# A gated decoder block: the positions' transfer, filler products, modulation rows, weight sums and gate constants in another order

## The chip, the core and the metric

One core of one Trainium2 chip runs the whole block as one program. TensorE (PE) multiplies, VectorE (DVE), ScalarE (ACT) and GpSimd (POOL) do elementwise work, and transfers between HBM and the core's SBUF are issued from the queues of SyncE (SP), ACT and POOL. Each engine takes its instructions strictly in the order of the program. The metric is the device time of one execution in microseconds.

## What is computed

The input is 2048 tokens of width 1024 in float32. Cut to what matters:

```python
c_act = silu(c)
shift, scale, gate = split(c_act @ w_ada + b_ada, 3)
h = rms(x, g_pre) * (1 + scale) + shift
q, k, v, z_a, u_b, v_b, z_b, g_logits = split(h @ w_in, ...)     # 4608 columns
q, k = rope(q, positions), rope(k, positions)
y_a = sliding_window_attention(q, k, v, sinks) * silu(z_a)       # window 128
y_b = gelu(u_b) * spatial_gating(layernorm(gelu(v_b))) * silu(z_b)
merged = sigmoid(g_a) * (y_a @ w_proj_a) + sigmoid(g_b) * (y_b @ w_proj_b)
out = x + gate * rms(merged @ w_out, g_post)
```

`rms` divides each token's row by its root mean square.

## The kernel before

The three large products (`w_in`, the two projections, `w_out`) are done by a two-level scheme of seven products in place of eight: an operand is cut into quarters A11, A12, A21, A22, and four sums of quarters, S1 = A21 + A22, S2 = S1 - A11, S3 = A11 - A21, S4 = A12 - S2, enter beside the quarters. Each quarter or sum is split into a high and a low half, and each product is three passes (high by high, high by low, low by high) of `mm3` (line 164). For a weight the high half is ACT's cast (line 212) and the low half DVE's subtraction (line 147). For an activation (the tiles T) ACT's copy (lines 638 and 640) makes the high half and DVE (lines 147 and 647) the low one.

`run_all` goes through the program in slots, one product of one block of weights to a slot. `later(n, f)` puts f a number of slots later, before or after that slot's product. Work on weights is a stream: `loads` are transfers, `sums` the sums of quarters, `preps` the casts. `want(n)` brings the stream up to cast n; before each cast it issues loads, makes the low half that is still due (`low_now`) and makes the sums up to that place. So the order on ACT and DVE follows from these calls, and each engine keeps it.

The first three blocks of weights (NFIRST) run together, product by product, so their first 21 slots are product 0 of block 0, 1, 2, then product 1 of block 0, 1, 2, and so on. Product 1 uses S1, product 2 uses S2, product 4 uses S3, product 5 uses S4. For these blocks `combos` makes the sums on DVE, for later ones on POOL. Each sum is also stored to HBM (`keep`), for the second half of the tokens.

Ahead of the first slot stands the prologue, for the first 512 tokens. `positions` spreads the positions over the partitions by a product with the identity (line 570, into bankY; the casts and copies for it are lines 568 and 569), and `rope_do(n)` does the next n of 25 steps on DVE that lead to sine and cosine. `squares` takes squares on ACT (536, 539) and sums them on DVE (153); `rstd` sums over partitions on TensorE (551, into bankZ), copies the result (554, DVE) and takes the inverse root on POOL (143, 144); `rstd_out` spreads it over the partitions (560, into bankW). `ada_row(0, kks)` multiplies the modulation weights of row kk (585), `ada_rows_out` copies the result (591, ACT), and `ada_fin` turns it (597, TensorE) and makes the factors A and offsets SH (603 to 606, DVE). Then come the activations (574, 640, 647) and the first `mm3`. `warm(n)` are filler products whose result nobody reads (425). Product 1's activations (T_365), those for tokens 512 to 1023, need a second norm and a second set of rows (`second_half`, after slot 2); `ada_fin(1)` stands in the middle of slot 3.

The sine and the cosine need another table on ACT (lines 510 and 518) than the GELU of line 745; each change is an ACT_TABLE_LOAD.

On ACT's queue the constants `col` and `cst` go out first (121, 128); the positions (449) stand behind the activation of line 419, which needs `col`. SP's queue carries the activations, the modulation weights and the first weights in this order, up to 40 us.

Late in the first product, with the second half of the tokens, `gate_end(h)` (slots 87 and 91) loads two rows of constants (1089, 1090) into buffers of the kind S, of which there are four, and lines 1099 and 1100 use them. In the same slots `o_step` (1069) loads pieces of `w_out` and has POOL make sums of them in S buffers, and attention loads its queries and keys (921, 924) for the scores of lines 940 and 941. There are ten buffers of the kind x.

Of the kernel before, what the change touches and what calls it, by code (L numbers as in the profile page):

```python
# [8 lines left out]
F32 = mybir.dt.float32  # L9
F32R = mybir.dt.float32r  # L10
I32 = mybir.dt.int32
# [8 lines left out]
NG = 4  # L20
# [35 lines left out]
def hybrid_block(ctx: ExitStack, tc: tile.TileContext, xt, x, wada, wgate, wI, wP, wO,  # L56
# [33 lines left out]
    def const(shape, name, dt=F32):  # L90
        return cp.tile(shape, dt, tag=name, name=name)
# [26 lines left out]


    col = const([P, 48], "col")[:, 0:NCOL]  # L120
    act.dma_start(col, colc)
# [78 lines left out]
    def w_get():  # L200
        n = taken[0]
        taken[0] += 1
        want(min(n + LA, max(2 * n - 2, NFIRST - 1)))
        if n + LA >= len(preps):
            low_now()
        w = ready[n]
        ready[n] = None
        return w
# [30 lines left out]
    def combos(env, n, first):  # L239

        def keep(i, t):
            if n is not None:
                later(1, lambda: sp.dma_start(sS[n][i], t))

        second = sub if first else psub

        def s13():
            s1 = env["S1"] = flat("S")
            if first:
                add(s1, env["A21"], env["A22"])  # L250
            else:
                psub(s1, env["A21"], env["A22"], ALU.add)
            second(env["A21"], env["A11"], env["A21"])
            keep(0, s1)
            keep(2, env["A21"])

        def s2():
            second(env["A11"], env["S1"], env["A11"])
            keep(1, env["A11"])

        def s4():
            low_now()
            second(env["A12"], env["A12"], env["A11"])
            keep(3, env["A12"])

        sums.extend([[], [s13, s2], [], [], [s4], [], []] if first else [[s13], [], [s2], [], [s4], [], []])
        preps.extend([lambda k=k: env[k] for k in ("A11", "S1", "A11", "A12", "A21", "A12", "A22")])

    def stream_fresh(quads, n=None):
# [4 lines left out]
        if first:  # L274
            plan.append((6, "A22", "raw"))
        for off, key, tag in plan:
            loads.append((at + off, fetch(env, key, quads[key], tag)))
        combos(env, n, first)
# [149 lines left out]
    adaw = [[T_new(F32).rearrange("p (a b) -> p a b", a=4) for _ in range(2)] for _ in range(2)]  # L428
    ropew = T_new(F32).rearrange("p (a b) -> p a b", a=8)
    rg = const([P, D], "rg")  # L430
# [16 lines left out]

    posi = ropew[0:NG, 7, :].bitcast(I32)
    act.dma_start(posi, pos)
    x_load(0)  # L450
# [209 lines left out]
    T[0], T[1] = t_new(), t_new()  # L660
    warm(2)
    positions()
    rope_do(6)
    squares(0, range(KT))
    warm(8)
    ada_row(0, range(0, 1))
    rstd(0, BK["Z"])
    ada_row(0, range(1, 2))
    rstd_out(0, BK["W"])
    rope_do(10)  # L670
    ada_row(0, range(2, 8))
    want(1)
    low_now()
    ada_load(1)
    cur["cap"] = 10
    ada_rows_out(0)
# [409 lines left out]
    def gate_end(h):  # L1086
        sl = slice(h * 512, (h + 1) * 512)
        bg, gp = flat("S"), flat("S")
        sp.dma_start(bg, rowc[0:1, sl].broadcast_to([P, 512]))
# [41 lines left out]
    def run_all():  # L1131
        nonlocal T

        for s in range(NS):
# [34 lines left out]
            if s == 0:  # L1169
# [4 lines left out]
                def second_half():  # L1174
                    rstd(1, BK["Z"])
                    ada_row(1, range(2))
                    rstd_out(1, BK["W"])
                    sum_to(NFIRST + 1)
                    want(NFIRST)
                    for i in range(6):  # L1180
                        t_part(1, i)
                        if i == 2:
                            low_now()
                    ada_row(1, range(2, 8))
                    ada_rows_out(1)
# [4 lines left out]
                later(2, second_half, True)  # L1190
                later(4, fetch_all, True)
                later(3, lambda: ada_fin(1), "mid")
# [201 lines left out]
```

## Time and profile before

| | us |
|---|---|
| median of 3 runs | 1241.12 |
| lowest and highest | 1240.72, 1242.14 |
| profiled execution, its own time | 1238.44 |
| its span, first to last instruction | 1236.7 |
| PE busy in the span | 1206.4 (98%) |
| DVE busy | 832.9 (67%) |
| ACT busy | 610.9 (49%) |
| POOL busy | 271.2 (22%) |

Times in the timeline count from the start of the span. A row gives start, duration, engine, line, operation, output and inputs by the program's names, and in brackets how long the engine stood before it and what ended that. "SPq" and "ACTq" are issues of transfers. A float32 product appears as passes: each filler of `warm` as two. "PEclk", the granted clock, is 1.00 at full speed and 0.50 at half.

### The profile page before, as it was taken

How to read it: one execution, taken by the hardware profiler on the slowest of the kernel's cores; microseconds unless marked ns; L12 is line 12 of the kernel's file. 1: busy time of each engine (PE TensorE's matmuls, PEld its weight loads, DVE VectorE, ACT ScalarE, POOL GpSimd, SP SyncE). 2: the span in 40 equal slices, each digit the busy share in tenths (PEclk: the TensorE clock that was granted, in tenths of full speed). 3: DMA queues.
4: the chain of work that ended last, by engine and by line, in shares of the span. 5: the costliest groups of instructions: out<-in, count | busy, mean ns of one | idle time of the engine just before them, and what ended most of it. 6: DMA issues, size and time to landing. Idle time of an engine off the chain costs nothing.

```text
span 1236.7 us, 17163 instructions
## 1 busy us (share of the span) xinstructions
PE 1206.4 (98%) x5500; PEld 960.7 (78%) x5500; DVE 832.9 (67%) x1290; ACT 610.9 (49%) x1324; POOL 271.2 (22%) x243
## 2 busy tenths in 40 slices
PE   8888999999999999999999999999999999999997
PEld 3566888887777777888888787777788888888886
DVE  5897688577777677348765775465746557677775
ACT  2366444576765667444344675455722112444443
POOL 0001556223465300013300001221000000135342
PEclk8999999999999999999999999999999999999999
DMA  9344898867999988468787666998787677754552
GB/s 362 128 138 146 296 335 295 257 180 218 279 334 342 316 294 281 141 217 290 263 278 199 175 171 186 332 282 257 263 290 237 223 244 242 266 184 143 164 179 85
DMA packets 215506, 294.15 MB, mean 238 GB/s; under 512 B 19828, under 2 KB 96244, under 8 KB 215416
## 3 DMA queue, kind: packets, MB, share of 16 engines
q1 hardware_dynamic: 214944, 292.37, 73.1%
q8 instruction: 43, 0.70, 0.2%
q0 software_dynamic: 176, 0.53, 0.2%
q14 instruction: 47, 0.39, 0.1%
q10 hardware_dynamic: 296, 0.16, 0.0%
HBM read 189.50 MB, written 98.24 MB: 233 GB/s over the span
## 4 chain that ended last, share of the span: by engine, by line
PE 86%; DVE 5%; DMA 4%; ACT 2%; issue 2%; SPq 1%; POOL 1%; DVEq 0%; ACTq 0%; POOLq 0%
PE bankY L164 27%; PE bankX L164 19%; PE bankZ L164 12%; PE bankW L164 12%; PE s L164 4%; PE b L164 4%; PE b L990 2%; PE s L940 1%; DMA T<-in_wada 1%; PE s L941 1%; PE b L879 1%; PE b L975 1%; DVE W L147 1%; DMA T<-in_xt 0%; DVE T L647 0%
## 5 line engine op out<-in xcount | busy, mean ns | idle before, releaser
L164 PE MATMUL bankY<-T,W 128*128 128x512 f32 x1608 | 390.4, 391 | 1.4 <-ACT bankZ L409 1.1
L164 PEld LDWEIGHTS bankY<-T,W 128*128 128x128 f32 x1608 | 299.5, 188 | 64.7 <-ACT bankZ L409 1.5
L147 DVE TENSOR_TENSOR W<-raw,W 128x512 fp32r<-128x512 f32 x323 | 237.7, 743 | 74.2 <-ACT W L212 72.1
L164 PE MATMUL bankX<-T,W 128*128 128x512 f32 x1140 | 279.4, 393 | 1.7 <-DVE T L647 1.3
L212 ACT CAST W<-raw 128x512 fp32r<-128x512 f32 x323 | 199.2, 617 | 152.2 <-PE b L164 48.4
L164 PEld LDWEIGHTS bankX<-T,W 128*128 128x128 f32 x1140 | 211.3, 188 | 47.4 <-DVE T L647 3.6
L164 PE MATMUL bankW<-T,W 128*128 128x512 f32 x708 | 177.9, 398 | 8.0 <-DVE W L147 3.7
L164 PE MATMUL bankZ<-T,W 128*128 128x512 f32 x708 | 173.2, 394 | 0.9 <-DVE W L147 0.9
L164 PEld LDWEIGHTS bankW<-T,W 128*128 128x128 f32 x708 | 132.3, 191 | 40.4 <-DVE W L147 4.2
L164 PEld LDWEIGHTS bankZ<-T,W 128*128 128x128 f32 x708 | 133.6, 190 | 29.2 <-DVE W L147 1.5
L150 POOL TENSOR_TENSOR S<-raw,raw 128x512 f32<-128x512 f32 x22 | 29.5, 1339 | 275.3 <-DMA raw<-m 201.3
L150 POOL TENSOR_TENSOR raw<-raw,raw 128x512 f32<-128x512 f32 x44 | 67.2, 1528 | 89.2 <-DVE W L147 42.1
L153 DVE TENSOR_TENSOR e<-bankY,e 128x512 f32<-128x512 f32 x41 | 28.3, 690 | 65.5 <-PE bankY L164 65.4
L147 DVE TENSOR_TENSOR T<-x,T 128x512 fp32r<-128x512 f32 (+1 forms) x93 | 64.5, 736 | 9.6 <-ACT T L364 9.1
L164 PE MATMUL s<-T,W 128*128 128x512 f32 x276 | 66.4, 389 | 0.0
L150 POOL TENSOR_TENSOR S<-x,x 128x512 f32<-128x512 f32 x18 | 26.1, 1459 | 182.6 <-DMA x<-in_wO 174.9
L150 POOL TENSOR_TENSOR raw<-S,raw 128x512 f32<-128x512 f32 x22 | 32.8, 1490 | 138.5 <-DVE W L147 115.1
L164 PEld LDWEIGHTS s<-T,W 128*128 128x128 f32 x276 | 51.7, 188 | 10.7
L364 ACT CAST T<-x 128x512 fp32r<-128x512 f32 x88 | 48.8, 618 | 4.2 <-PE s L164 4.2
L969 ACT ACTIVATE P<-P,rc 128x128 f32<-128x128 f32 x128 | 44.4, 396 | 11.3 <-DVE rc L965 11.0
L409 ACT COPY bankZ<-bankY 128x512 f32<-128x512 f32 x42 | 24.0, 570 | 52.7 <-PE bankY L164 52.6
L388 ACT COPY e<-bankW 128x512 f32<-128x512 f32 x41 | 24.0, 584 | 52.1 <-PE bankW L164 49.5
(233 smaller groups left out, 1405.3 us busy)
## 6 DMA issues: line engine op xcount, KB each, us to landing
raw<-in_wI SPq DMA_DIRECT2D x128, 256.0 KB, 4.6
raw<-sS SPq DMA_DIRECT2D x84, 256.0 KB, 4.6
g<-e SPq DMA_DIRECT2D x64, 256.0 KB, 4.4
sS<-raw SPq DMA_DIRECT2D x48, 256.0 KB, 4.0
T<-in_wada SPq DMA_DIRECT2D x16, 512.0 KB, 8.1
q<-q SPq DMA_DIRECT2D x64, 128.0 KB, 5.2
q<-k_s SPq DMA_DIRECT2D x64, 128.0 KB, 4.7
raw<-in_wP SPq DMA_DIRECT2D x32, 256.0 KB, 3.3
```

The costliest lines, as they stand in the source:

```text
L147: dve.tensor_tensor(out=o, in0=a, in1=b, op=ALU.subtract)
L150: pool.tensor_tensor(out=o, in0=a, in1=b, op=op)
L153: dve.tensor_tensor(out=o, in0=a, in1=b, op=ALU.add)
L164: pe.matmul(o, w[:, i, sl], t[:, j, kt, :], start=start and kt == kts[0] and n == 0, stop=stop and kt == last and n == 2, skip_group_check ...
L212: act.copy(w[:, 0, :], src)
L364: act.copy(T[p][:, 0, kt, :], rs[kt])
L388: act.copy(self.wsb, b["W"])
L409: act.copy(self.b[to], self.b[of])
L879: pe.matmul(b[:, ch * P : (ch + 1) * P], st["v", h][:, ch, :], wT[:, c, :], start=True, stop=True)
L940: pe.matmul(o, q[:, g, :], k[:, 0, :], start=True, stop=False)
L969: act.activation(out=st["P", kv][:, g, 0:P], in_=st["P", kv][:, g, 0:P], func=AF.Copy, scale=st["rc", kv][:, g : g + 1])
L990: pe.matmul(o[own, :], v[:, k, own], st["pv", kv][k], start=k == 1, stop=k == 0)
```

## The change

Six things are edited; no arithmetic is added or dropped.

1. The positions' transfer becomes the first on ACT's queue, ahead of `col` and `cst`; its tile is allocated earlier, so tiles carry other numbers.
2. Three fillers stand before the positions' product and six after it, instead of two and eight.
3. Two more rope steps follow the squares, and eleven instead of ten follow the norm: 19 of the 25 are done before the first product instead of 16.
4. Three modulation rows instead of two stand before `rstd_out`.
5. For the first three blocks S1 is made first for all of them, ahead of product 1's activations; S2 and S3, which were made with it, follow with products 1 to 4. S2 no longer overwrites A11 but A22, which makes A22 be loaded again under the name A22b, and S3 overwrites A21 later. `w_get` makes the due low half at once for casts 3 to 5, `want(NFIRST + 1)` is called inside the making of product 1's activations, and two limits on loads (`cap`, `fetch_all`) change.
6. `gate_end` takes x buffers instead of S.

```diff
+    ropew = T_new(F32).rearrange("p (a b) -> p a b", a=8)
+    posi = ropew[0:NG, 7, :].bitcast(I32)
+    act.dma_start(posi, pos)
     col = const([P, 48], "col")[:, 0:NCOL]
     act.dma_start(col, colc)
...
         want(min(n + LA, max(2 * n - 2, NFIRST - 1)))
+        if NFIRST <= n < 2 * NFIRST:
+            low_now()
...
-        def s13():
-            s1 = env["S1"] = flat("S")
-            if first:
-                add(s1, env["A21"], env["A22"])
-            else:
-                psub(s1, env["A21"], env["A22"], ALU.add)
+
+        two = "A22" if first else "A11"
+
+        def s1():
+            env["S1"] = flat("S")
+            (add if first else lambda o, a, b: psub(o, a, b, ALU.add))(env["S1"], env["A21"], env["A22"])
+            keep(0, env["S1"])
+
+        def s3():
             second(env["A21"], env["A11"], env["A21"])
-            keep(0, s1)
             keep(2, env["A21"])
 
         def s2():
-            second(env["A11"], env["S1"], env["A11"])
-            keep(1, env["A11"])
+            env["S2"] = env[two]
+            second(env["S2"], env["S1"], env["A11"])
+            keep(1, env["S2"])
...
-        sums.extend([[], [s13, s2], [], [], [s4], [], []] if first else [[s13], [], [s2], [], [s4], [], []])
+        sums.extend([[], [s1], [s2], [], [s3], [s4], []] if first else [[s1, s3], [], [s2], [], [s4], [], []])
...
-            plan.append((6, "A22", "raw"))
+            plan.append((6, "A22b", "raw"))
...
-    posi = ropew[0:NG, 7, :].bitcast(I32)
-    act.dma_start(posi, pos)
...
-    warm(2)
+    warm(3)
     positions()
     rope_do(6)
     squares(0, range(KT))
-    warm(8)
+    rope_do(2)
+    warm(6)
     ada_row(0, range(0, 1))
     rstd(0, BK["Z"])
-    ada_row(0, range(1, 2))
+    ada_row(0, range(1, 3))
     rstd_out(0, BK["W"])
-    rope_do(10)
-    ada_row(0, range(2, 8))
+    rope_do(11)
+    ada_row(0, range(3, 8))
...
-    cur["cap"] = 10
+    cur["cap"] = 8
...
-        bg, gp = flat("S"), flat("S")
+        bg, gp = flat("x"), flat("x")
...
-                    sum_to(NFIRST + 1)
+                    sum_to(2 * NFIRST)
                     want(NFIRST)
                     for i in range(6):
                         t_part(1, i)
                         if i == 2:
                             low_now()
+                        elif i == 4:
+                            want(NFIRST + 1)
...
-                later(4, fetch_all, True)
+                later(3, fetch_all, True)
```

TensorE in the prologue, before; line 425 is the filler, 570 the positions' product, 585 the modulation rows (two instructions each), 551 the norm's partition sums, 560 its spreading:

```order
L425 MATMUL bankX<-ones 128x512 x2
L570 MATMUL bankY<-T_320 128x512
L425 MATMUL bankX<-ones 128x512 x8
L585 MATMUL b_408<-T_316,cact 64x512 x2
L551 MATMUL bankZ<-ones,e_377 128x2 x4
L585 MATMUL b_408<-T_316,cact 64x512 x2
L560 MATMUL bankW<-cst,rs_417 128x128 x4
L585 MATMUL b_408<-T_316,cact 64x512 x4
L585 MATMUL b_408<-T_317,cact 64x512 x8
```

The same place now, the lines being 436, 578, 593, 559 and 568:

```order
L436 MATMUL bankX<-ones 128x512 x3
L578 MATMUL bankY<-T_291 128x512
L436 MATMUL bankX<-ones 128x512 x6
L593 MATMUL b_409<-T_318,cact 64x512 x2
L559 MATMUL bankZ<-ones,e_378 128x2 x4
L593 MATMUL b_409<-T_318,cact 64x512 x4
L568 MATMUL bankW<-cst,rs_418 128x128 x4
L593 MATMUL b_409<-T_318,cact 64x512 x2
L593 MATMUL b_409<-T_319,cact 64x512 x8
```

One filler has moved ahead of the positions' product and one is gone; one row has moved from behind the spreading to before it.

DVE after product 1's last activation, before; 153 and 147 on S and raw are the sums of blocks 1 and 2, 603 to 606 the second factors, 147 on W the weights' low halves, 574 the scaling of product 2's activations:

```order
L147 TENSOR_TENSOR T_365<-Tt,T_365 128x512
L153 TENSOR_TENSOR S_625<-raw_497,P_499 128x512
L147 TENSOR_TENSOR raw_497<-raw_352,raw_497 128x512
L147 TENSOR_TENSOR raw_352<-S_625,raw_352 128x512
L153 TENSOR_TENSOR S_631<-raw_501,S_503 128x512
L147 TENSOR_TENSOR raw_501<-raw_354,raw_501 128x512
L147 TENSOR_TENSOR raw_354<-S_631,raw_354 128x512
L603 TENSOR_TENSOR AS<-b_648,col 128x4
...
L147 TENSOR_TENSOR W_629<-S_625,W_629 128x512
L147 TENSOR_TENSOR W_667<-S_631,W_667 128x512
L574 SCALAR_TENSOR_TENSOR x_325<-x_325,AS,e_586 128x512
```

The same place now (W_614, W_663 are the weights of blocks 1 and 2 for product 1, W_669 that of block 0 for product 2, P_497 and P_501 are S2 of blocks 0 and 1):

```order
L150 TENSOR_TENSOR T_365<-Tt,T_365 128x512
L150 TENSOR_TENSOR W_614<-S_592,W_614 128x512
L611 TENSOR_TENSOR AS<-b_643,col 128x4
...
L150 TENSOR_TENSOR P_497<-S_590,raw_350 128x512
L150 TENSOR_TENSOR W_663<-S_594,W_663 128x512
L150 TENSOR_TENSOR P_501<-S_592,raw_352 128x512
L150 TENSOR_TENSOR W_669<-P_497,W_669 128x512
L582 SCALAR_TENSOR_TENSOR x_326<-x_326,AS,e_588 128x512
```

Six sums have gone from between the activations and the factors; two other sums and the subtraction for W_669 have come ahead of the scalings.

ACT at that place, before; 638 and 212 are casts of activations and weights, 591 copies the second modulation rows, 388 and 409 copy banks after product 1 of block 0:

```order
L638 CAST T_365<-Tt 128x512
L591 COPY e_623<-b_577 128x512
L212 CAST W_629<-S_625 128x512
L388 COPY m_663<-bankW 128x512
L409 COPY bankW<-bankX 128x512
L212 CAST W_667<-S_631 128x512
L212 CAST W_672<-raw_350 128x512
```

And now:

```order
L646 CAST T_365<-Tt 128x512
L217 CAST W_614<-S_592 128x512
L599 COPY e_629<-b_579 128x512
L399 COPY m_658<-bankW 128x512
L420 COPY bankW<-bankX 128x512
L217 CAST W_663<-S_594 128x512
L217 CAST W_669<-P_497 128x512
```

The cast of block 1's weights has moved ahead of the copy of the rows; the cast of block 2's stands where it stood, behind the two copies of banks.

Further on, ACT's sine comes during product 3 and its cosine during product 4, instead of products 4 and 5, so that four table loads follow the first one instead of five. On SP's queue the instructions around `gate_end` keep their order; only the buffers' names change, from S to x.

More of the change, by code (lines that the diff above doesn't have):

```diff
@@ L245, in combos, with last @@
         second = sub if first else psub
-        def s13():
-            s1 = env["S1"] = flat("S")
-            if first:
-                add(s1, env["A21"], env["A22"])
-            else:
-                psub(s1, env["A21"], env["A22"], ALU.add)
+        two = "A22" if first else "A11"
[4 more added lines that the diff above has]
+        def s3():
             second(env["A21"], env["A11"], env["A21"])
-            keep(0, s1)
             keep(2, env["A21"])
         def s2():
-            second(env["A11"], env["S1"], env["A11"])
-            keep(1, env["A11"])
+            env["S2"] = env[two]
+            second(env["S2"], env["S1"], env["A11"])
+            keep(1, env["S2"])
         def s4():
             low_now()
-            second(env["A12"], env["A12"], env["A11"])
+            second(env["A12"], env["A12"], env["S2"])
             keep(3, env["A12"])
-        sums.extend([[], [s13, s2], [], [], [s4], [], []] if first else [[s13], [], [s2], [], [s4], [], []])
-        preps.extend([lambda k=k: env[k] for k in ("A11", "S1", "A11", "A12", "A21", "A12", "A22")])
+        def last():
+            return env["A22b"] if first else env["A22"]
+        sums.extend([[], [s1], [s2], [], [s3], [s4], []] if first else [[s1, s3], [], [s2], [], [s4], [], []])
+        preps.extend([lambda k=k: env[k] for k in ("A11", "S1", "S2", "A12", "A21", "A12")] + [last])
     def stream_fresh(quads, n=None):
@@ L274, in stream_fresh @@
         if first:
-            plan.append((6, "A22", "raw"))
+            plan.append((6, "A22b", "raw"))
         for off, key, tag in plan:
-            loads.append((at + off, fetch(env, key, quads[key], tag)))
+            loads.append((at + off, fetch(env, key, quads[key[:3]], tag)))
         combos(env, n, first)
@@ L428, in hybrid_block @@
     adaw = [[T_new(F32).rearrange("p (a b) -> p a b", a=4) for _ in range(2)] for _ in range(2)]
-    ropew = T_new(F32).rearrange("p (a b) -> p a b", a=8)
     rg = const([P, D], "rg")
```

## The prediction

> **What bounds the kernel now.** I read the page first, then the waits, then the timeline of the stretches in which TensorE stands. From the page, the span and the chain of work that ended last:
>
> ```profile
> span 1236.7 us, 17163 instructions
> ...
> PE 86%; DVE 5%; DMA 4%; ACT 2%; issue 2%; SPq 1%; POOL 1%; DVEq 0%; ACTq 0%; POOLq 0%
> ```
>
> TensorE sets the end. The change leaves out no product, so it can gain only where TensorE does not yet run its products back to back (the first 118 us), or stands later. The list of waits, TensorE only, from 110 us to the end (waited for; us in total, times, longest), has five entries; the longest:
>
> ```profile
> PE s L940 <- DMA q<-k_s: 2.5, 1, 2.5
> ```
>
> It is one wait of 2.5 us, and it is of interest below. All else is decided before 118 us. The timeline there (start, duration, engine, line, in brackets the idle time before):
>
> ```profile
> 1.11 3.51 PE L425 MATMUL bankX<-ones 128*128 128x512 f32 x4 [1.11 <-DVE nhalf L126]
> ...
> 3.84 0.51 ACTq L449 DMA_DIRECT2D T<-in_pos  x1
> ...
> 7.39 0.42 DVE L568 CAST T<-T 4x512 f32<-4x512 int32 x1 [2.94 <-DMA T<-in_pos]
> ...
> 7.99 2.07 PE L570 MATMUL bankY<-T 4*128 4x512 f32 x2 [3.38 <-DVE T L569]
> ...
> 9.99 9.33 PE L425 MATMUL bankX<-ones 128*128 128x512 f32 x16
> 10.10 0.75 DVE L461 TENSOR_SCALAR T<-bankY,col 128x512 f32<-128x512 f32 x1 [2.16 <-PE bankY L570]
> ...
> 13.34 5.46 DVE L153 TENSOR_TENSOR e<-e,m 128x512 f32<-128x512 f32 x7
> ...
> 19.25 1.08 PE L585 MATMUL b<-T,cact 128*64 128x512 f32 x4
> ...
> 20.26 1.05 PE L551 MATMUL bankZ<-ones,e 128*128 128x2 f32 x8
> ...
> 21.35 0.16 DVE L554 COPY ss<-bankZ 128x4 f32<-128x4 f32 x1 [2.55 <-PE bankZ L551]
> ...
> 23.50 1.16 PE L560 MATMUL bankW<-cst,rs 128*128 128x128 f32 x8 [1.18 <-POOL rs L144]
> ...
> 24.59 5.37 PE L585 MATMUL b<-T,cact 128*64 128x512 f32 x24
> ...
> 30.01 0.59 ACT L591 COPY e<-b 128x512 f32<-128x512 f32 x1 [3.69 <-PE b L585]
> ...
> 31.74 0.16 DVE L603 TENSOR_TENSOR AS<-b,col 128x4 f32<-128x4 f32 x1 [2.93 <-PE b L597]
> ```
>
> It is one chain: positions land, a matmul spreads them, DVE does six rope steps and seven sums of squares (10.10 to 18.80), TensorE sums over partitions (20.26), POOL takes the root, TensorE spreads it (23.50), the last six modulation rows follow, and only then (31.74) are there weights for the activations.
>
> **The positions' transfer.** Now it is issued at 3.84, behind an activation that waits for the constants. First on the queue it goes out some 3 us earlier, and the two other transfers one place (0.45 us) later. From the table of DMA issues (size, us from issue to landing):
>
> ```profile
> cst<-in_consts ACTq DMA_DIRECT2D x1, 128.0 KB, 4.2
> col<-in_colc ACTq DMA_DIRECT2D x1, 21.0 KB, 3.0
> ```
>
> The spreading matmul also needs the identity out of the constants: issued at 1.7, plus 4.2, is 5.9; the small copy and the step to TensorE took 0.6 (7.39 to 7.99, the cast in it), of which 0.3 is left. So 6.2. Three fillers instead of two take 3/2 of 3.51, 5.27 us, and end at 6.38. The matmul starts at 6.4 instead of 7.99: 1.6 earlier (1.0 to 2.2 if the constants land later, or the clock rises within the filler).
>
> **The matmul itself, and the clock.** It took 2.07 us. Windows of 3.41 us (us, TensorE busy, instructions, granted clock, DMA):
>
> ```profile
> 11.01:14.43 3.42, 3.42 (x6) 0.50 1.03 418
> ...
> 21.25:24.67 3.42, 2.24 (x15) 1.00 1.05 386
> ...
> 55.39:58.80 3.41, 2.41 (x14) 1.00 0.01 2
> 58.80:62.21 3.41, 3.41 (x10) 0.50 0.09 18
> ...
> 92.93:96.35 3.42, 1.84 (x6) 1.00 0.42 134
> 96.35:99.76 3.41, 3.41 (x10) 0.50 1.01 324
> ```
>
> The clock halves at an edge of such a window after 1.84 us of work in it; after 2.41 us too, where 1.1 us of that were two-column products; not after 2.24 us of other work. It comes back one window later. In the old prologue TensorE stood 3.38 us, and the clock was 0.50 until 14.43. The new one works from 1.11 on without that hole, so I take the full clock for this matmul: 1.05 us (2.07 is the other end). Then rope and sums, 8.70 as before: they end at 6.4 + 1.05 + 8.7 = 16.2 (17.2 at half clock), not 18.80.
>
> **Less filler.** Now the filler holds TensorE until 19.25, and a row until 20.33, though the sums were there at 18.80. A pass takes 0.44 at full clock (16 passes: 4.44 us at half clock for five, 4.89 for eleven). Twelve passes end at 12.8, the row at 13.9. TensorE then waits 2.3 us for DVE: a new wait, but the sums now decide. The partition sums start at 16.2 instead of 20.26.
>
> **Two rows moved ahead of the spreading, two rope steps ahead of DVE's copy.** The copy needs the partition sums (1.05) and now two rope steps (2/6 of 3.24, 1.08): they lie beside each other, nothing. From copy to spreading passed 2.15 (21.35 to 23.50), in which TensorE did one row of 1.08 and stood 1.18; two rows take 2.16. Five rows are left after it instead of six: 5/6 of 5.37 is 4.48, a gain of 0.9. So from the start of the partition sums 1.09 + 2.15 + 1.09 + 4.48 = 8.8 instead of 9.7: the rows end at 25.0 at full clock, not 29.96, 4.95 earlier. Two covers have to hold. The modulation weights must be there; on the chain of waits their first half is
>
> ```profile
> 9.16 9.34 DMA T<-in_wada
> ```
>
> and ends at 18.5, before row three. And DVE must be free: eleven rope steps and two weight subtractions last 8.0 from the copy (ten took 7.4, till 28.80), to 25.5, before the new 26.8 of line 603. What is late next is the clock. Idle 2.3 plus 1.05 us of two-column products is a whole window with little work, so I expect a fall there; half speed for 3.4 us costs 1.7 of work, of which some 0.3 falls into the idle time. I take 1.4 off: **3.5 earlier**; ends 4.95 (no fall) and 1.5 (two windows, 3.4). The first product's steps then only shift: their data stood ready, and the weight sums after it come at 42 instead of 45.62, when the transfers are over (DVE's timeline; then a window, its last figures the DMA share and GB/s):
>
> ```profile
> 45.62 0.69 DVE L153 TENSOR_TENSOR S<-raw,P 128x512 f32<-128x512 f32 x1
> ...
> 40.00:42.00 2.00, 2.00 (x10) 1.66 (x9) 1.92 (x3) 0.00 (x0) 0.00 (x0) 1.00 0.39 144
> ```
>
> One rule bears on this step. The Trainium skill, "TensorE: Matmul & The Clock Gate" (section "Why this matters for your kernels"), says that only idle gaps above about 3 us, a whole window, bring the half clock. By it the 1.4 would not be lost. The trace disagrees: it fell after a window with 2.41 us of work.
>
> **The deferred weight sums.** In the second product (same columns):
>
> ```profile
> 57.33 0.58 ACT L591 COPY e<-b 128x512 f32<-128x512 f32 x1
> ...
> 57.96 1.12 PE L597 MATMUL b<-cst,e 128*128 128x2 f32 x8 [1.00 <-ACT e L591]
> ...
> 61.89 0.59 ACT L388 COPY m<-bankW 128x512 f32<-128x512 f32 x1 [2.48 <-PE bankW L164]
> ...
> 62.99 0.62 ACT L212 CAST W<-S 128x512 fp32r<-128x512 f32 x1
> ...
> 64.25 1.41 DVE L574 SCALAR_TENSOR_TENSOR x<-x,AS,e 128x512 f32<-128x512 f32 x2
> ...
> 91.85 1.28 ACT L510 ACT_TABLE_LOAD   x1
> ...
> 109.30 1.79 DVE L147 TENSOR_TENSOR x<-x,rg 128x512 f32<-128x512 f32 x1
> ```
>
> Six sums leave DVE's stretch from 58 to 62. It does not get ahead by them: in its order the subtraction for the third block's weights now stands ahead of the scalings, and their high half is ACT's cast of 62.99, behind the copy at 61.89, which waits for TensorE. ACT has a new cast ahead of its copy of 57.33, so all that is 0.5 later. After the cast (now to 64.1) come three DVE steps of about 0.6: the scalings start at 65.9 instead of 64.25, 1.7 later (0.4 if the clock does not fall at 58.8: from 59.1 to 61.9 TensorE ran at half speed). The sums left out come back one to a slot, where the old order had as many. Against it: three rope steps (3 x 0.54) are gone into DVE's idle 2.93 before 31.74, and ACT saves one table load of 1.28 (order: five now after the first, four then). TensorE meets the weights of the next block earlier, yet waits for the activations. I put the net at **0.3 later**; ends 1.0 earlier, and 2.0 later if POOL's sums, which come earlier, fall upon DVE here: beside them a DVE step took 1.79 instead of 0.71 (half of 1.41).
>
> **Gate constants in other buffers.** SP's queue and who waits, from the timeline:
>
> ```profile
> 760.20 0.53 SPq L1089 DMA_DIRECT2D S<-in_rowc  x1
> 772.22 0.34 SPq L1090 DMA_DIRECT2D S<-in_rowc  x1
> ...
> 771.50 0.69 DVE L1099 TENSOR_TENSOR rg<-b,S 128x512 f32<-128x512 f32 x1 [1.54 <-PE b L1095]
> ...
> 785.26 1.20 SPq L924 DMA_DIRECT2D q<-k_s  x2
> ...
> 790.90 0.35 PE L940 MATMUL s<-q,q 128*128 128x256 f32 x1 [2.48 <-DMA q<-k_s]
> ```
>
> SP stood at line 1090 from 760.7 to 772.2, for the buffer that DVE's line 1099 had to read first. All 20 transfers behind it were late, the last of them the keys for which TensorE stood 2.48 us. With x buffers, of which ten exist, neither load waits for a reader; SP goes on 11 us earlier, and the keys land well before 788. I take **2.4 earlier**, ends 0 and 2.5.
>
> **The sum.** 3.5 - 0.3 + 2.4 = 5.6 us. The profiled execution took 1238.44 (span 1236.7 and 1.7 around it); it would be 1232.8. The median of the runs is 1241.12, 2.7 above it; the same difference gives 1235.5. The ends: 4.95 + 1.0 + 2.5, 1232.7; and 1.5 - 2.0, 1241.6.
>
> **Rivals.** *The clock does not fall* in the prologue: 1.4 more, 1234.1. For it: a window with 2.24 us of work kept it; against: the two-column window. Chance 0.13. So it would go by the rule of the Trainium skill's "TensorE: Matmul & The Clock Gate" named above.
> *TensorE waits at 788 anyway*, for the queries or a weight: 1241.12 - 3.2 = 1237.9. For it: SP has other waits there; against: each is short, and no other wait of TensorE is near. 0.10.
> *The first gain is swallowed*: from 58 to 118 TensorE follows DVE and ACT, and the new order there loses 3 us more, by ACT's cast and POOL: about 1238.7. For it: DVE is full there; against: its steps are fewer. 0.11.
> *Slower:* the half clock stays from the wait on, through the rows and the first product. Rows at twice the time (2.2 + 4.5), the products another 6: with 5.0 and 2.4 gained it is 5 us slower, 1246. It decides if a window filled with rows does not lift the clock. Against: at 24.59 rows kept it at 1.00, and both falls quoted lasted one window. 0.06.
>
> **How the numbers follow.** The forecast, 1235.5, has 0.60. What a measurement can tell from no change is 0.2%, 2.5 us: faster means below 1238.6. The forecast gives 0.58 of that, the clock rival 0.13, the second rival 0.08, the third 0.03: 0.82. Slower 0.06, the same 0.12. The range, 1232.9 to 1239.0, leaves out the slower rival, the upper end of the third, and 0.05 to 0.08 below.
>
> **What would show it.** The spreading matmul near 6.4; partition sums near 16 to 17.5; rows ending near 26 (25 with the clock at 1.00, later than 28 wrong); what was line 603 near 28; no scaling in the second product earlier than the shift; SP's two loads side by side near 755 and no wait of TensorE on the keys there. It is wrong if the rows end where they did, if the third product ends no earlier than before, or if TensorE stands elsewhere between 750 and 800.

## The result, and the profile after

| | before | after |
|---|---|---|
| median of 4 runs, us | 1240.92 | 1231.63 |
| lowest and highest, us | 1240.26, 1242.14 | 1230.65, 1232.23 |
| profiled execution, us | 1238.44 | 1232.23 |
| its span, us | 1236.7 | 1230.5 |

The ratio is 0.9923, with a 95% interval of 0.9906 to 0.9940: 9.3 us faster, where 5.6 were forecast. The time lies 1.3 us below the forecast range. The profiled execution, however, came near its forecast: 1232.23, where the sum had given 1232.8. That is the first thing to explain.

Span and chain of the kernel after:

```profile
span 1230.5 us, 17163 instructions
...
PE 89%; DVE 6%; ACT 2%; issue 2%; DMA 1%; POOL 1%; ACTq 0%; DVEq 0%; SPq 0%; POOLq 0%
```

The timeline of the prologue (start, duration, engine, line, in brackets the idle time before and what ended it), and of the table of DMA issues the constants:

```profile
5.61 0.41 DVE L576 CAST T<-T 4x512 f32<-4x512 int32 x1
...
7.70 0.21 DVE L577 COPY T<-cst 4x128 f32<-4x128 f32 x1 [1.68 <-DMA cst<-in_consts]
7.97 1.96 PE L578 MATMUL bankY<-T 4*128 4x512 f32 x2 [2.25 <-DVE T L577]
...
9.86 7.92 PE L436 MATMUL bankX<-ones 128*128 128x512 f32 x12
...
18.72 1.05 PE L559 MATMUL bankZ<-ones,e 128*128 128x2 f32 x8
...
23.06 4.51 PE L593 MATMUL b<-T,cact 128*64 128x512 f32 x20
...
28.25 1.05 PE L605 MATMUL b<-cst,e 128*128 128x2 f32 x8
...
29.34 0.16 DVE L611 TENSOR_TENSOR AS<-b,col 128x4 f32<-128x4 f32 x1 [1.47 <-PE b L605]
```

```profile
cst<-in_consts ACTq DMA_DIRECT2D x1, 128.0 KB, 5.9
```

The positions are there at 5.61, earlier than the 7.39 of before. But the constants now land at 7.7, after 5.9 us instead of 4.2, and the product that needs both starts at 7.97, as it did. TensorE still stands before it, the clock is at half from 8.12 to 14.94, and the six fillers (12 passes) take 7.92; in an execution at full speed, shown below, they take 5.42. With the row behind them they hold TensorE until the squares are summed (18.67), and so hide the wait that I had put there. What is won is shorter filler and one row less: 28.25 instead of 30.64.

SP's queue at the gate, and the longest wait of TensorE after 110 us (waited for; us in total, times, longest):

```profile
755.99 0.59 SPq L1098 DMA_DIRECT2D x<-in_rowc  x1
756.62 0.43 SPq L1099 DMA_DIRECT2D x<-in_rowc  x1
768.44 1.21 SPq L933 DMA_DIRECT2D q<-k_s  x2
```

```profile
PE s L949 <- ACT P L969: 1.2, 1, 1.2
```

The two loads stand side by side, the keys that had been issued at 785.26 go out at 768.44, and the wait for them is gone.

One new wait is the longest of the kernel. The fifth product (slots 12 to 14), timeline:

```profile
87.63 1.28 ACT L526 ACT_TABLE_LOAD   x1
88.92 0.63 ACT L526 ACTIVATE T<-T 128x512 f32<-128x512 f32 x1
89.46 0.60 ACT L217 CAST W<-raw 128x512 fp32r<-128x512 f32 x1
...
90.09 0.69 DVE L150 TENSOR_TENSOR W<-raw,W 128x512 fp32r<-128x512 f32 x1 [2.44 <-ACT W L217]
...
92.70 2.10 PE L167 MATMUL bankW<-T,W 128*128 128x512 f32 x5 [4.33 <-DVE T L655]
...
94.61 3.96 PE L167 MATMUL bankZ<-T,W 128*128 128x512 f32 x12
```

The last rope step is a sine on ACT. Its table load stands ahead of a cast of weights; DVE stands 2.44 us for that cast, with the subtraction, a sum of weights and the activations' steps (line 655 the last) behind it; TensorE stands 4.33 us, and then runs at half speed (3.96 for 12 passes that take 2.9).

**A table of all traces.** The experiments below are read with two numbers from TensorE's timeline: where the product of line 597 (605 after, other numbers in other kernels) starts, at the prologue's end, and how long it takes from there to the end of the first 21 slots, the last `s` of the seventh product. For the kernel after the rows are the 28.25 above and

```profile
116.83 2.88 PE L167 MATMUL s<-T,W 128*128 128x512 f32 x12
```

so 119.71 - 28.25 = 91.46. In the same way:

| kernel | prologue's end | from there to the end of slot 20 | median | ratio to before, interval |
|---|---|---|---|---|
| before, first profile | 30.64 | 93.23 | 1240.92 | |
| before, second profile | 31.80 | 92.49 | 1241.90 | 1.0008 (0.9997, 1.0019) |
| gate alone | 31.85 | 93.08 | 1236.88 | 0.9966 (0.9953, 0.9978) |
| deferral alone | 31.09 | 96.20 | 1245.30 | 1.0033 (1.0021, 1.0045) |
| after | 28.25 | 91.46 | 1231.63 | 0.9923 (0.9906, 0.9940) |
| after without deferral | 28.84 | 90.48 | 1231.45 | 0.9926 (0.9909, 0.9942) |
| after, positions late | 29.77 | 91.60 | 1233.56 | 0.9941 (0.9925, 0.9956) |
| after, old prologue | 30.41 | 97.00 | 1238.81 | 0.9981 (0.9972, 0.9989) |
| after, 16 rope steps | 26.43 | 94.81 | 1234.95 | 0.9957 (0.9942, 0.9973) |
| after, small identity | 26.39 | 91.96 | 1230.99 | 0.9918 (0.9905, 0.9930) |
| after, sines together, late | 29.58 | 92.76 | 1233.52 | 0.9938 (0.9925, 0.9951) |
| after, sines early | 28.81 | 88.43 | 1229.36 | 0.9906 (0.9887, 0.9925) |
| sines early, small identity | 26.09 | 87.33 | 1226.38 | 0.9883 (0.9865, 0.9902) |
| the same without deferral | 28.31 | 86.99 | 1226.51 | 0.9880 (0.9858, 0.9901) |

An interval is some 1 to 2.5 us to either side; where two overlap, the traces have to speak. Each ratio is to runs of before beside the kernel: the experiments were run in three groups, with medians of before of 1240.89, 1240.66 and 1241.38, and the kernel after ahead of them. Below I take differences of medians; taken through the ratios' groups they change by at most 0.5 us.

### The profile page after: what moved, and what is told of

It reads as the page before. It is cut to its first block, busy times and chain, and to the rows that moved or that the text cites. A ratio compares the mean times of both kernels' runs of the same rounds, so it can differ in the third digit from the quotient of the medians.

```text
span 1230.5 us, 17163 instructions
## 1 busy us (share of the span) xinstructions
PE 1203.1 (98%) x5498; PEld 958.1 (78%) x5498; DVE 829.2 (67%) x1290; ACT 609.6 (50%) x1323; POOL 270.1 (22%) x243
## 4 chain that ended last, share of the span: by engine, by line
PE 89%; DVE 6%; ACT 2%; issue 2%; DMA 1%; POOL 1%; ACTq 0%; DVEq 0%; SPq 0%; POOLq 0%
PE bankY L167 28%; PE bankX L167 19%; PE bankZ L167 12%; PE bankW L167 12%; PE s L167 4%; PE b L167 4%; PE b L999 2%; PE s L949 1%; PE s L950 1%; PE b L984 1%; DVE W L150 1%; PE b L888 1%; PE bankX L436 1%; DVE T L655 1%; DVE T L150 0%
## 5 line engine op out<-in xcount | busy, mean ns | idle before, releaser
L150 DVE TENSOR_TENSOR W<-raw,W 128x512 fp32r<-128x512 f32 x320 | 234.3, 739 | 75.5 <-ACT W L217 75.5
L167 PE MATMUL bankW<-T,W 128*128 128x512 f32 x708 | 175.1, 395 | 7.9 <-DVE T L655 6.3
```

The source lines that it names most:

```text
L150: dve.tensor_tensor(out=o, in0=a, in1=b, op=ALU.subtract)
L167: pe.matmul(o, w[:, i, sl], t[:, j, kt, :], start=start and kt == kts[0] and n == 0, stop=stop and kt == last and n == 2, skip_group_check ...
```

## The experiments

**The gate constants alone.** In the kernel before:

```diff
-        bg, gp = flat("S"), flat("S")
+        bg, gp = flat("x"), flat("x")
```

> The kernel before with the gate constants alone in x buffers. Prediction: the wait of 2.48 us on the keys near 788 us is gone, nothing else moves; 2.4 us below the kernel before. Rival, TensorE waits there anyway for something else: within 0.5 us of the kernel before. Second rival, the gap of 9.3 us between the two medians holds some 3 us that the profiled executions (6.2 apart) do not show, and the buffers are what removes them: 5 us or more below.

Measured 1236.88 beside 1240.89, 4.0 us (2.7 to 5.8 by the interval): more than the 2.48 us that the first profile showed. The next run tells why.

**The kernel before once more**, nothing edited.

> The kernel before once more, unchanged, for its profile and the spans of several executions. The profiled execution had been 2.7 us below the median of the timed ones. Theory that this is scatter from one execution to the next inside the first 125 us (half-clock windows that fall at other places): spans between 1236.5 and 1240.5, this profile's stretch ahead of 125 us longer or shorter by 1 to 3 us than the first profile's, the rest alike. Rival, the difference lies outside the span: spans all near 1236.7, and times 3 to 5 us above them. Second rival, it lies later than 125 us, at the wait near 788 us: that wait is 2.5 us in one profile and 4 to 6 in the other.

Measured 1241.90 (1238.80 to 1243.84); 18 runs of before beside these four kernels lay between 1238.44 and 1244.42, and the first profiled execution, 1238.44, is the lowest of them. The second profile's span, the wait on the keys in it, and windows from the edge at which the clock fell (us, TensorE busy, PEld, DVE, ACT, POOL, granted clock, DMA share, GB/s):

```profile
span 1241.6 us, 17163 instructions
```

```profile
792.94 0.55 PE L940 MATMUL s<-q,q 128*128 128x256 f32 x1 [4.06 <-DMA q<-k_s]
...
794.79 4.31 PE L164 MATMUL bankW<-T,W 128*128 128x512 f32 x12
```

```profile
790.94:794.35 3.41, 1.41 (x6) 1.44 (x7) 0.69 (x1) 0.00 (x0) 1.28 (x2) 0.50 1.04 381
794.35:797.77 3.42, 3.42 (x10) 2.75 (x10) 2.33 (x5) 0.00 (x0) 0.00 (x0) 0.50 1.08 326
797.77:801.18 3.41, 3.41 (x16) 2.81 (x15) 0.69 (x1) 1.82 (x6) 0.00 (x0) 1.00 1.07 355
```

Here the wait is 4.06 us instead of 2.48, and the clock is at half for two windows of 3.41 us, which begin within the wait and hold 4.83 us of work. The gate kernel's profile has the same prologue to 0.05 us and a span of 1235.4, 6.2 below; it has no wait there. From the start of line 990's product ahead of the wait to the first bankX product behind it 15.09 us pass in this execution (786.94 to 802.03), 11.26 in the first profile (786.48 to 797.74) and 8.76 in the gate kernel (787.54 to 796.30). So the wait with what follows costs 6.3 us here and 2.5 in the first. What scatters is mainly the keys' transfer: TensorE starts 6.88 us after its issue (786.06 to 792.94), in the first profile 5.64 (785.26 to 790.90). Two windows of the gate kernel at this place, at full speed:

```profile
791.00:794.00 3.00, 3.00 (x15) 2.48 (x14) 2.00 (x5) 0.58 (x2) 0.00 (x0) 1.00 0.94 301
794.00:797.00 3.00, 3.00 (x17) 2.51 (x16) 1.11 (x2) 2.10 (x8) 0.00 (x0) 1.00 1.08 360
```

So the second rival of that expectation holds for most of the difference: of the 4.9 us between the two spans 3.8 lie at this one wait. The prologue's 1.2 (30.64 and 31.80) have shrunk to 0.4 by the end of slot 20. The rival of the gate run, that the medians' extra is in what the buffers remove, holds for some 1.5 us: the 4.0 measured lie between the 2.5 and the 6.3 of the two executions. Before's runs spread over 6 us, seven of the gate kernel over 1.7 (1235.83 to 1237.49). But the wait is not all that scatters: the kernel with sixteen rope steps (below), which lacks it too, spreads over 4.8 us in eight runs.

**After without the deferral.** The weight sums, the limits on loads and the calls in product 1's activations as before:

```diff
-        sums.extend([[], [s1], [s2], [], [s3], [s4], []] if first else ...
+        sums.extend([[], [s13, s2], [], [], [s4], [], []] if first else ...
...
-                later(3, fetch_all, True)
+                later(4, fetch_all, True)
```

> The changed kernel with the weight sums of the first blocks as they were before (S1, S2 and S3 together, the old limits on loads), so the prologue and the gate buffers remain. Prediction as it was written, the deferral costs 0.3 us: 0.3 below the changed kernel. Reading of the two traces, the deferral won 1.65 us between 54 and 124 us: 1.7 above the changed kernel, 4.9 (2.4 of the prologue and 2.5 of the gate) below the kernel before in its trace. If the medians' extra 3 us also hang on this stretch: 4 to 5 us above the changed kernel.

Measured 1231.45, 0.2 us below the kernel after. Beside the rest of the change no worth of the deferral is seen, as the prediction's 0.3 had it, though the two intervals leave room for 2 us or more; the 1.7 read from the first pair of traces did not come. Product by product (lengths from the ends of the `s` rows) the kernel after is 2.4 us shorter in the second and 0.5 in the third, 2.0, 1.2 and 1.5 longer in the fourth to sixth, and 0.8 shorter in the seventh: won first, given back as the sums come one to a slot.

**The deferral alone**, in the kernel before.

> The kernel before with the deferred weight sums alone. Prediction: 0.3 us slower than the kernel before, and the run without the deferral, which equalled the changed kernel, says the same: within 1 us of the kernel before. Rival, from the first pair of traces (1.65 us won between 54 and 124 us): 1.7 us faster.

Measured 1245.30, 4.6 us slower than before. Both expectations fell: the same edit costs 0.2 us, not told from 0, in one surrounding and 4.6 in the other. The stretch in the table says the same, 96.20 against 92.49, and 91.46 against 90.48. What is different in the surroundings is tried in the next two.

**Positions late again**, in the kernel after: the issue goes back behind the activation.

```diff
-    act.dma_start(posi, pos)
     col = const([P, 48], "col")[:, 0:NCOL]
...
+    act.dma_start(posi, pos)
     x_load(0)
```

> The changed kernel with the positions' transfer back behind the activation of the third queue, all else as changed. Prediction as written, the early transfer is worth 1.6 us: the spreading product starts at 8 us or later instead of 6.4 and the kernel is 1.2 to 1.6 us slower than the changed one. Reading of the trace after, in which the product started at 7.97 because the constants landed at 7.7: the constants land earlier again (5.9 or 6 us), the positions at 7.4, the product starts at 8.0 as before, and the time is within 0.3 us of the changed kernel.

Measured 1233.56, 1.9 us slower by the medians, though the intervals overlap. The timeline there:

```profile
8.31 0.41 DVE L576 CAST T<-T 4x512 f32<-4x512 int32 x1 [3.79 <-DMA T<-in_pos]
...
8.92 1.24 PE L578 MATMUL bankY<-T 4*128 4x512 f32 x2 [2.36 <-DVE T L577]
```

The product starts 0.95 us later than in the kernel after, not at the same time. The first profile of before, with 7.99, was an early one; the second has 8.64, the gate kernel 8.68, the kernel with the deferral alone 8.61. In the six traces with the early transfer and the constants as they were it starts between 6.67 and 7.97. On average the transfer brings the product about 1 us forward, not 0 and not 1.6: from there on the constants hold it.

**The old prologue**, in the kernel after (its transfer, deferral and gate kept), and **sixteen rope steps** with the new fillers and rows:

```diff
-    warm(3)
+    warm(2)
...
-    rope_do(2)
-    warm(6)
+    warm(8)
     ada_row(0, range(0, 1))
     rstd(0, BK["Z"])
-    ada_row(0, range(1, 3))
+    ada_row(0, range(1, 2))
     rstd_out(0, BK["W"])
-    rope_do(11)
-    ada_row(0, range(3, 8))
+    rope_do(10)
+    ada_row(0, range(2, 8))
```

```diff
-    rope_do(2)
     warm(6)
...
-    rope_do(11)
+    rope_do(10)
```

> The changed kernel with fillers, rope steps and rows of the prologue as before (two and eight fillers, six and ten rope steps, two rows ahead of the spreading), the positions' transfer still first. Prediction's steps: the fillers hold TensorE past the end of the squares again (1.6 us: partition sums at 20.3 instead of 18.7), six rows instead of five follow (0.9), and three rope steps come back into the later slots; 2.5 to 3.5 us slower than the changed kernel. Rival, the early transfer alone carries the prologue's gain: within 0.7 us of the changed kernel.

> The changed kernel with sixteen rope steps ahead of the first product instead of nineteen (none behind the squares, ten behind the norm); fillers, rows, transfer and the rest as changed. With sixteen, ACT loads its table five times after the first (sine, GELU, sine, GELU around the slots of both), with nineteen four times, and the last three steps fall into the slots of the sixth and seventh product. If it is the rope steps that made the old prologue 7 us slower: 4 to 5 us slower than the changed kernel. Rival, fillers and rows made it: within 1.5 us of the changed kernel.

Measured 1238.81 and 1234.95: 7.2 and 3.3 us slower than the kernel after; the first is twice what was expected, the second lies between its two expectations. Nearly half of what the old prologue costs is not fillers or rows, but three rope steps of 0.4 to 0.7 us on DVE, and ACT's functions behind them, that come back into the later slots. (The sixteen-step kernel's prologue ended at 26.43 in its profile, an early one; its stretch behind it is 3.35 longer.) Where they cost, sixth product, timeline of the kernel with sixteen:

```profile
100.08 1.28 ACT L526 ACT_TABLE_LOAD   x1
...
101.37 0.63 ACT L526 ACTIVATE T<-T 128x512 f32<-128x512 f32 x1
103.17 0.75 DVE L655 SCALAR_TENSOR_TENSOR T<-x,AS,T 128x512 fp32r<-128x512 f32 x1 [1.72 <-ACT T L648]
103.18 0.50 PE L167 MATMUL bankX<-T,W 128*128 128x512 f32 x1 [1.55 <-ACT T L648]
```

The second sine falls one product later, ahead of the activations of the sixth, which takes 13.00 us instead of 10.22, a half-clock window in it. Without the deferral no run changes the rope steps alone. The stretch of the gate kernel, which has sixteen steps and the whole old prologue, is 2.6 us longer than that of the kernel after without the deferral (93.08 and 90.48), the second profile of before 2.0; if all of that is the steps, they explain only 1 us or so of what the deferral alone costs. In the trace of that run two half-clock stretches are two windows long (59.08 to 65.91 and 96.63 to 103.46), one in the second profile of before each; why they came there is not settled, and so the 4.6 is not either.

**A small transfer for the identity**, in the kernel after, with nine fillers behind the product:

```diff
     act.dma_start(posi, pos)
+    id4 = const([P, 16], "id4")[0:NG, 0:NG]
+    act.dma_start(id4, consts[0:NG, 0:NG])
...
-    dve.tensor_copy(..., ident[0:NG, 0:NG, None].broadcast_to([NG, NG, 32]))
+    dve.tensor_copy(..., id4[:, :, None].broadcast_to([NG, NG, 32]))
...
-    warm(6)
+    warm(9)
```

> The changed kernel with the four rows and columns of the identity that the positions' product needs in a small transfer of their own, second on the queue, and nine fillers instead of six behind the product. If the constants' landing at 7.7 us is what holds the product at 7.97: it starts near 6.3, the squares end 1.7 us earlier, and the kernel is 1 to 1.7 us faster than the changed one. Rival, the sums end earlier but the clock or the modulation weights take the gain: within 0.5 us.

Measured 1230.99, 0.6 below the kernel after, which this measurement does not tell from 0. In the trace the copy for the product no longer waits for the constants, the product starts at 6.88 and the prologue ends at 26.39, 1.9 earlier; the span is 2.0 shorter. That the constants held the product in the kernel after is shown (its row at 7.70); that the gain comes out whole is not.

**Both sines behind slot 14**, in the kernel after: `rope_steps` makes both arguments first, then sine and cosine, and

```diff
-                for n in range(5, 15):
-                    later(n, lambda n=n: rope_do(1 if n < 14 else 26), True)
+                for n in (5, 6, 7, 8, 9, 14):
+                    later(n, lambda n=n: rope_do(1 if n < 14 else 26), True)
```

> The changed kernel with the sine and the cosine evaluated one after the other behind slot 14 instead of behind slots 7 and 10, so that ACT loads the table for them once instead of twice. In the trace of the changed kernel a table load at 87.6 us and the activation behind it hold ACT's weight cast, DVE stands 2.44 us for that, TensorE 4.33, and a half-clock window follows (1.7 us). If that is so, both go: 3 to 6 us faster than the changed kernel. Rival, DVE is the bound of that stretch and the wait comes back at another place: within 1 us.

Measured 1233.52, 1.9 slower by the medians, with overlapping intervals. The wait of 4.33 fell to 2.40, and the fifth product from 14.49 to 11.08 us. But the sixth and seventh, in whose midst the table load now stands, are 3.6 us longer: the rival. The prologue of this execution is of use too:

```profile
7.30 1.12 PE L578 MATMUL bankY<-T 4*128 4x512 f32 x2 [0.70 <-DVE T L577]
8.35 5.42 PE L436 MATMUL bankX<-ones 128*128 128x512 f32 x12
13.70 1.08 PE L593 MATMUL b<-T,cact 128*64 128x512 f32 x4
17.21 1.70 PE L559 MATMUL bankZ<-ones,e 128*128 128x2 f32 x8 [2.44 <-DVE e L156]
```

It has the kernel after's instructions. The constants landed earlier, the fillers ran at full speed, and here is the wait that the prediction put at 2.3 us, with the half clock behind it, from 17.42 to 24.25 (the partition sums take 1.70 instead of 1.05). That is two windows. From the partition sums to the prologue's end 12.37 us pass, in the kernel after, at full speed, 9.53. The prologue ends at 29.58, later than the 28.25 of the execution without the wait.

**The sines early**, in the kernel after:

```diff
                 def second_half():
+                    rope_do(3)
                     rstd(1, BK["Z"])
+                    rope_do(3)
                     ada_row(1, range(2))
...
-                for n in range(5, 15):
-                    later(n, lambda n=n: rope_do(1 if n < 14 else 26), True)
```

> The changed kernel with the six rope steps that remain after the prologue taken out of slots 5 to 10: three in front of the second norm's copy on DVE, three behind it, where DVE stood 1.97 and 2.20 us in the trace of the changed kernel; sine and cosine follow on ACT there, which stood 10.5 us, and ahead of the first GELU, so that two table loads go. If ACT's table load and DVE's rope steps make the waits of the fifth product (4.33 us and a half-clock window): 4 to 7 us faster than the changed kernel. Rival, as with both behind slot 14, the wait comes back elsewhere: within 1.5 us.

Measured 1229.36, 2.3 below the kernel after; its profile had the wait and the half clock in the prologue. ACT loads the table while it stands anyway, and the wait of the fifth product is a third of what it was:

```profile
36.78 1.28 ACT L518 ACT_TABLE_LOAD   x1
42.83 0.63 ACT L518 ACTIVATE T<-T 128x512 f32<-128x512 f32 x1 [4.77 <-DVE T L471]
44.96 0.63 ACT L526 ACTIVATE T<-T 128x512 f32<-128x512 f32 x1 [1.50 <-DVE T L471]
```

```profile
90.24 1.61 PE L167 MATMUL bankW<-T,W 128*128 128x512 f32 x5 [1.44 <-DVE T L655]
```

The stretch to the end of slot 20 is 88.43 instead of 91.46. Of the 4 to 7 us expected 3.0 came in the stretch and 2.3 in the median, whose intervals overlap; the next pair gives it more sharply. The rope steps on DVE and the table loads moved together here; the run before divides them. There the steps on DVE stayed in their slots, ACT's load alone moved out of the fifth product (from 87.63 to 103.61), that product became 3.4 us shorter and the two around the load longer. So the wait of the fifth product is the load's.

**Early sines with the small identity, with the deferral and without.**

> The same with the small transfer of the identity and nine fillers. The two gains add: 0.6 us below the kernel with the early sines (the small transfer alone was 0.6 below the changed kernel). Rival, the small transfer's 1.1 to 1.4 us in the trace come out whole: 1.4 below.

> The same as the kernel with early sines and the small transfer, but with the weight sums as before the change. If the deferral is neutral (with it and without it the changed kernel came to 1231.6 and 1231.5): within 0.7 us of it. If the deferral's sums cost in the slots where the rope steps had been, and the gain of the first slots stays (2.4 us won in the second product, 4.7 lost in the fourth to sixth by the traces): with the rope steps gone the deferral pays, and this kernel is 1 to 3 us slower.

Measured 1226.38 and 1226.51. Both beat the kernel after beyond their intervals (0.9883 up to 0.9902, against 0.9923 down to 0.9906) and before by 15 us. The first of the two differs from the kernel with the small identity by the early sines alone: 4.6 us by the medians, with intervals that do not touch (0.9902 and 0.9905), and 4.6 in the stretch (91.96 and 87.33). So the worth of the early sines is shown. The small identity and its fillers add 3.0 to the early sines, more than either expectation, though these intervals overlap: nine fillers also cover the wait of 2.44, and the profile of the first of the two shows the full clock throughout. Of the deferral again no worth is seen (0.1).

## Why the prediction was wrong

- **The failed step: the terms were read from one execution, and 2.7 us were added to carry them to the median.** I added the 2.7 us by which the median of before stood above its profiled execution, as if every version carried them. They are scatter of what the change removes, of the wait on the keys most of all (3.8 of the 4.9 us between the two profiles of before), and 1238.44 was the lowest of 18 executions. By terms, the gate was priced 1.6 us too low and the prologue with its rope steps 1.9 (the bullets below); these make up the miss.
- **That the profiled executions agree (1232.8 and 1232.23) is luck in part.** Between these two traces the gate gave 2.5 (2.4 forecast) and the prologue's end 2.4 (3.5 forecast); the stretch behind it became 1.8 shorter, where 0.3 longer was forecast. The last two misses nearly cancel. The profile of before was its lowest execution, that of the kernel after the highest of its four.
- **The gate: right mechanism, wrong size.** 2.4 with an upper end of 2.5, taken from one execution's wait. Measured 4.0. The wait is 2.48 in one profile, 4.06 with two half-clock windows behind it in the next (6.3 us in all), and 3.38 with one in the kernel with the deferral alone. A profile's wait is a draw, and its end is not an upper bound.
- **The positions' transfer: 1.6 forecast, about 1 measured.** The step that failed is the constants' landing: I had taken their 4.2 us from the row of before. With the positions late they took 4.0 to 4.6 us in five traces, with the positions ahead of them 4.6 to 5.9.
- **Fillers and rows: right in sum.** From the partition sums to the end of the rows 8.8 were forecast; 18.72 to 27.57 is 8.85. The profiled execution had neither the wait nor the fall of the clock. In the six traces with six fillers there is a wait in five (0.74 to 2.44 us) and a fall behind it in four. From the partition sums to the prologue's end 9.53 us pass at full clock, 10.8 with one half-clock window (two traces) and 12.2 to 12.4 with two (two traces): 1.3 for one window, as the 1.4 forecast had it, but 2.7 to 2.8 for two. The prologue's end moved 2.4 to 3.55 us, by which of before's profiles one takes; 3.5 were forecast. On average over the four traces with the old prologue and the five with the new one and the early transfer it moved 3.0.
- **The rope steps: the second mis-sized term.** I let three steps and one table load vanish in the net of the weight sums. They are worth 3.3 us in the medians with the deferral, and at most 2.0 to 2.6 in the traces without it. That is more than their 1.6 us on DVE. The rows of the sixth product put it on ACT's table load ahead of an activation, and the run with both sines behind slot 14, which moved a load and no step on DVE, says the same of the fifth.
- **The weight sums: right in size, in part by luck.** 0.3 later forecast, 0.2 measured between the two runs, which is not told from 0. The scalings did start 0.3 after the shift (64.25 - 2.39 is 61.86), where 0.4 was forecast for the full clock, and the clock did not fall there:

```profile
62.13 1.41 DVE L582 SCALAR_TENSOR_TENSOR x<-x,AS,e 128x512 f32<-128x512 f32 x2
```

But the second product won 2.4 and the later ones gave it back, which I had not seen. Nor had I seen that the same edit costs 4.6 us with the old prologue; why it does stays open.
- **What this sums to.** 4.0 of the gate, 5.4 of the prologue with its rope steps (1236.88 to 1231.45) and -0.2 of the sums make 9.2 of the 9.3 measured. The three differences run through one row of kernels (before, gate alone, after without the deferral, after), so that they add up is no proof. Of the rivals, the clock stayed up behind the squares in the profiled execution, but not for the reason given: fillers at half speed left no wait there. The other three did not come.

## What to carry to other kernels

Before a profile's wait is priced, ask how it scatters: take the kernel's profile a second time, and never carry the offset between a profile and a median over to a version that lacks the wait. A table load on ACT costs what stands behind it in the queue; put functions of another table where that engine stands idle, in one piece. The worth of an edit that fills slots depends on what else is in them (none seen, or 4.6 us lost, here), so try it with and without its neighbours.

## What the runs showed of the hardware

**The clock.** Half-clock stretches begin and end on a grid of 3.41 us, and where the grid lies against the first instruction differs from execution to execution: in the two profiles of before one began at 58.82 and at 60.49. Windows laid on the grid, from the kernel with the old prologue and then from the kernel after:

```profile
68.96:72.37 3.41, 1.77 (x7) 0.97 (x6) 3.41 (x7) 2.50 (x5) 0.00 (x0) 1.00 0.02 5
72.37:75.78 3.41, 3.30 (x9) 2.16 (x8) 3.20 (x6) 2.46 (x5) 0.00 (x0) 0.50 0.01 4
106.51:109.92 3.41, 1.33 (x5) 0.55 (x4) 1.69 (x4) 3.38 (x6) 0.00 (x0) 1.00 0.33 102
109.92:113.33 3.41, 3.41 (x8) 2.72 (x9) 2.73 (x4) 2.42 (x4) 1.21 (x1) 0.50 1.01 347
```

```profile
62.73:66.14 3.41, 1.76 (x8) 0.91 (x6) 3.41 (x7) 1.42 (x3) 0.00 (x0) 1.00 0.24 71
66.14:69.55 3.41, 2.15 (x7) 1.19 (x8) 3.28 (x6) 2.71 (x6) 0.00 (x0) 1.00 0.02 5
```

I laid all fourteen traces out so, from 4 to 125 us and from where the record of the clock begins (in two of them at 16 us). Every window at full clock with at most 1.51 us of work was followed by half clock; windows of 1.56 to 1.90 sometimes (the one of 1.56, from the kernel with the positions late, was not); above that only windows with two-column products or the positions' four-row product in them, up to 2.51. Where a wait lies on the grid thus decides whether up to 1.7 us more are lost to each half-clock window behind it. The Trainium skill, "TensorE: Matmul & The Clock Gate" (section "Part 1: The HAM clock gate"), says that the window runs free and does not start with the kernel, so that the same kernel meets it in another phase each run; the traces agree. The same page's rule (section "Why this matters for your kernels") that idle gaps above about 3 us bring the half clock back is not the whole of it here: in the window from 106.51 no gap was longer than 1.55 us, and the clock fell. TensorE's longest gap in it:

```profile
109.07 0.49 PE L167 MATMUL bankX<-T,W 128*128 128x512 f32 x1 [1.55 <-ACT T L648]
```

**The table load** on ACT took 1.28 us in each row above. The Trainium skill, "ScalarE: Activation LUTs" (section "What ACT_TABLE_LOAD costs"), gives the same for the load, and 1.4 us more of draining; no such time shows here, where the load began at 87.63, 0.02 us after the activation before it had ended, and the sine at 88.92, 0.01 us after the load's end.
